# Low weight parts on GpSimd, values by DMA, decay in the keys, and longer pauses in a two-layer hybrid decoder step

## The chip, the cores and the metric

The kernel runs on one core of one Trainium2 chip. The metric is the device time of one execution in microseconds; the time of a kernel is the median of its runs. The core's engines are named as in the profile: PE is TensorE's matrix products, PEld its weight loads, DVE is VectorE, ACT is ScalarE, POOL is GpSimd and SP is the engine that issues most of the DMAs. Each engine works through its own queue in order.

## The reference

The reference is one inference step of two decoder layers for a prompt of 512 tokens and 8 samples of 4 tokens, which share the weights: 544 tokens in all, 1024 channels. A layer does the following (cut to what matters here):

```python
h = rmsnorm(x, norm1_g) * (1 + scale1) + shift1
z = h @ w_in                       # columns for four mixers and for four merge gates
yA = pool_mixer(z_A)               # causal means over 2, 4, 8, 16 tokens
yB = retention(z_B)                # rotary queries and keys, decay, chunks of 128
yC = B * conv3(C * h_c)            # short gated convolution
yD = rwkv7_mixer(z_D)              # the scan, below
mixed = sum(sigmoid(z_gate[n]) * (y[n] @ w_br[n]) for n in A, B, C, D) @ w_out
x = x + gate1 * mixed
h2 = rmsnorm(x, norm2_g) * (1 + scale2) + shift2
up = causal_dwconv3(h2 @ w_up)
x = x + gate2 * ((silu(up_a) * up_b) @ w_down)
```

The scan of branch D carries one 64 x 64 state per head over the tokens, for 4 heads:

```python
def step(S, inp):
    rt, wt, kt, vt, at, bt = inp
    S = S * wt + (S @ at)[:, None] * bt + vt[:, None] * kt     # decay, delta rule, value x key
    return S, S @ rt
```

Besides the output rows the step returns the new states of every mixer.

## The kernel before

Channels lie on the 128 partitions, tokens along the free dimension. The 544 tokens are worked in two halves of 272 columns (`HS`), so one weight block of 128 x 128 multiplies 272 columns at a time.

**The weight stream.** All large weights of a layer come in 138 units (`NU`) of 128 x 1024, in the order in which they are used: 8 units for branch D's input (`RW_UNITS`), 6 for branch C (`SC_UNITS`), 10 for branch C's gates and projection, 2 for branch A (`PO_UNITS`), 10 for A's gates, 8 for branch B (`RET_UNITS`), 10 for D's gates, 10 for B's gates, 8 for the output projection, and the rest for the feed-forward part. Units 0 to 63 are the mixing weights. `load_unit` (L104) fetches a unit by DMA into `raw` (three buffers), lets ScalarE round it to a high part `whi` (L113) and lets VectorE subtract to get the low part `wlo` (L114); two units of layer 0 have this subtraction on GpSimd. `getw` calls it two or three units ahead of their use. Activations are split in the same way (`split_hilo`). `mm3` then forms three products for each block: high by high (L133), high by low (L134), low by high (L135), into a PSUM bank of the pool `psd` (three banks).

**The planner.** The order of TensorE's instructions is written out by hand: it is the order of the program. The other engines' instructions are put in order by a scheduler that knows priorities. Work with small matmuls (the branch D mixer `rwkv`, retention, the conditioning products `ada`, the norms) is written as Python generators. After each `mm3` the function `slot` looks which generators are due; a generator says by `yield n` after how many more of the large products it wants to go on. So a pause is a number of large products; as `slot` is asked after every third, a pause of 16 lasts 18.

**Branch D.** `rwkv` first forms decays and keys (L404 to L450). `products(T)` makes, for each block of 128 tokens, the scaled keys `bkv` (L481) and the scaled `LG` (L473, L475) on VectorE, with a few columns copied by GpSimd (L474); five blocks follow one another at pauses of 48 and 44. In each, small matmuls turn the keys (L500, into `BK`) and multiply them (L507). A triangular system is solved by substitution on VectorE (L568 to L580) and comes back through DRAM into `XT`. Then the scan runs over 16 chunks of 32 tokens. A chunk has three steps, parted by the pauses `D_G`, `D_S` and `D_P`:

1. a matmul with the state and values `Z` (L653), whose result four copies bring to `gs` (two on ScalarE, two on VectorE, L615);
2. a matmul with `XT` (L620), whose result four copies write into `Z` (L624); `newZ` (L600) prepares the `Z` of the next pair of chunks: GpSimd clears blocks and VectorE copies the values `vT` into their places, 32 x 64 each (L607);
3. the matmuls of the new state (L673) and the outputs (L677); VectorE adds the decayed old state `Pn` (L685), multiplies by the decay `dec` and writes the halves into `Z` (L691); GpSimd forms `Pn` for the next chunk (L692).

Behind the scan come the 8 x 4 sample tokens (L712 to L751), a norm over each head (L759, L383 to L391) and the split that the projection of branch D's gates reads (L775, L395). The retention of branch B starts when the scan is done (`M["scan_done"]`).

**The ends of the two halves of a layer.** `residual` (L341) adds a product to the stream `x`: VectorE reads the PSUM bank for the prompt columns (L346) and, in the second half, for the 32 sample columns (L350), whose result `t` stands in a buffer of the pool `zr`. That pool has ten buffers of 562 columns and serves nearly every intermediate: norms, gates, convolutions, keys.

Where the merge gates run, `gates` lets ScalarE take the sigmoid of a unit's product (L1129), VectorE multiply the projected branch by it (L1111) and GpSimd or VectorE add it up (L1113).

Of the kernel before, what the change touches and what calls it, by code (L numbers as in the profile page):

```python
# [10 lines left out]
F32 = mybir.dt.float32  # L11
# [13 lines left out]
NU = 138  # L25
D_G, D_S, D_P = 12, 12, 18
KAPPA = -math.exp(-0.5)
# [16 lines left out]
def tile_hybrid_step(ctx: ExitStack, tc: tile.TileContext, io: dict):  # L44
# [11 lines left out]
    t4p = ctx.enter_context(tc.tile_pool(name="t4p", bufs=14))  # L56
    zrp = ctx.enter_context(tc.tile_pool(name="zrp", bufs=10))
    wp = ctx.enter_context(tc.tile_pool(name="wp", bufs=4))
    drp = ctx.enter_context(tc.tile_pool(name="drp", bufs=2, space=bass.MemoryType.DRAM))
# [6 lines left out]
    def ZR(n=562, dt=F32):  # L66
        return zrp.tile([128, n], dt, tag="zr", name=nm("zr"))

    def PM():
# [34 lines left out]
    def load_unit(l, u):  # L104
        raw = wp.tile([128, 1024], F32, tag="raw", name=nm("raw"), bufs=3)
        nc.sync.dma_start(raw, io["wst"][l, u])
        dst = extra_pools.get((l, u))
        if dst is None:
            hi = wp.tile([128, 1024], F32R, tag="whi", name=nm("whi"))
            lo = wp.tile([128, 1024], F32R, tag="wlo", name=nm("wlo"))  # L110
        else:
            hi, lo = dst()
        S.copy(hi, raw)  # L113
        (G if (l, u) in ((0, 1), (0, 2)) else V).tensor_tensor(out=lo, in0=raw, in1=hi, op=SUB)  # L114
        wloaded[(l, u)] = (hi, lo)
# [225 lines left out]
    def residual(xt, m, ps, half, gate):  # L341
        c0, c1 = HS[half]
        npc = HALF if half == 0 else SEQ - HALF
        x = xk(xt, m)
        with tc.high_priority():
            V.scalar_tensor_tensor(out=x[:, c0:c0 + npc], in0=ps[:, :npc], scalar=gate[:, m, 0:1], in1=x[:, c0:c0 + npc],  # L346
                                   op0=MUL, op1=ADD)
            if half == 1:
                t = ZR(32)
                V.tensor_tensor(out=smp(t), in0=smp(ps[:, npc:HALF]),  # L350
                                in1=gate[:, m, 1:9].unsqueeze(2).broadcast_to([128, NB, DT]), op=MUL)
        if half == 1:
            V.tensor_tensor(out=x[:, SEQ:TOK], in0=x[:, SEQ:TOK], in1=t, op=ADD)
        return x[:, c0:c1]
# [42 lines left out]
    def rwkv(l, za, zb, M, yD):  # L397
# [51 lines left out]
        def products(T):  # L449
# [29 lines left out]
            for w, src in enumerate((kkb, za)):  # L479
                for p in range(2):  # L480
                    V.tensor_tensor(out=bkv[:, p, :, w ^ p, :], in0=src[:, 2 + p, t0:t0 + n].rearrange("p (c t) -> p c t", t=32),  # L481
                                    in1=Ei[:, p, :].rearrange("p (c t) -> p c t", t=32), op=MUL)
            return bkv

        bkn = products(0)
        yield 48, True
        for T in range(5):
            n = 128 if T < 4 else 32
            nch = n // 32
            bkv = bkn  # L490
            if T < 4:
# [3 lines left out]
            for c in range(nch):  # L495
                for p in range(2):
                    cc = (c * 2 + p) * 64
                    for q in range(2):
                        r = par_rows(q)
                        PE.matmul(psB[kv_rows(q), cc:cc + 64], lhsT=bkv[r, p, c].rearrange("r w t -> r (w t)"),  # L500
                                  rhs=ident[r, 64 * q:64 * q + 64], start=True, stop=True)
# [21 lines left out]
            if T < 4:  # L523
                yield 44, True
        rks = []
# [74 lines left out]
        def newZ(blocks):  # L600

            Z = [M["pool"].tile([128, 2, 2, 64], F32, tag=f"z{q}", name=nm("z"), bufs=2) for q in range(2)]
            for q in range(2):
                for p in range(2):
                    G.memset(Z[q][b_rows(q, p), :, p, :], 0.0)
                    for c, (vT, j) in enumerate(blocks):
                        V.tensor_copy(Z[q][k_rows(q, p), c, p, :], vT[32 * j:32 * j + 32, p, q, :])  # L607
            return Z
# [31 lines left out]
        for q in range(2):  # L640
            G.memset(Z[q][par_rows(q), 0], 0.0)
        Pn = None
        P0 = None
        g0s = None
        yield 42
        for ch in range(16):
# [28 lines left out]
            for p in range(2):  # L675
                for q in range(2):
                    PE.matmul(pY[par_rows(q), p, 32 * c:32 * c + 32], lhsT=Z[q][:, c % 2, p, :], rhs=LG[q][:, ch, p, r_cols(q)],  # L677
                              start=True, stop=True)
            pP = psP[:, 0:128].rearrange("r (p i) -> r p i", p=2)
            db = dec[:, :, ch:ch + 1].broadcast_to([128, 2, 64])  # L680
            Pt = M["pool"].tile([128, 2, 64], F32, tag="pt", name=nm("pt"), bufs=2)
            if Pn is None:
                V.tensor_copy(Pt, pP)
            else:
                V.tensor_tensor(out=Pt, in0=pP, in1=Pn, op=ADD)  # L685
            Pn = M["pool"].tile([128, 2, 64], F32, tag="pn", name=nm("pn"), bufs=2)
            if ch < 15:
                Zt, cn = (Z, 1) if c % 2 == 0 else (Zn, 0)
                for q in range(2):
                    r = par_rows(q)  # L690
                    V.tensor_tensor(out=Zt[q][r, cn], in0=Pt[r], in1=db[r], op=MUL)  # L691
            G.tensor_tensor(out=Pn, in0=Pt, in1=db, op=MUL)  # L692
            if c == 3:
# [3 lines left out]
            if ch == 14:  # L697
                psG0 = PM()
                g0v = psG0[:, 0:128].rearrange("r (p w b t) -> r p w b t", p=2, w=2, t=DT)
                for p in range(2):  # L700
                    for b in range(NB):
                        for q in range(2):
# [3 lines left out]
                                      start=True, stop=True)  # L706
                g0 = ZR(128)
                S.copy(g0, psG0[:, 0:128])
# [71 lines left out]
    def retention(l, p, rt, M, yB):  # L780
# [36 lines left out]
        for T in range(4):  # L817
            for q in range(2):
                PE.matmul(pst[par_rows(q), 64 * T:64 * T + 64], lhsT=kt[:, T, par_rows(q)], rhs=vt[:, T, par_rows(q)],
                          start=True, stop=True)  # L820
        sms_s = ZR(32)
        V.tensor_tensor(out=sms_s[0:64], in0=ps[0:64, 0:32], in1=cst[0:64, C_RETS:C_RETS + 32], op=MUL)
        vks = ZR(128)
        S.copy(vks[0:64], pv[0:64, 0:128])
# [744 lines left out]
```

## Time and profile before

| | |
|---|---|
| median of 3 runs | 1979.79 us (1979.74 to 1980.87) |
| the profiled execution | 1977.9 us |
| its span | 1976.1 us |
| granted TensorE clock, mean over the span | 0.99 |
| DMA, mean over the span | 115 GB/s |

The profile is of one execution. A row of a timeline names start, duration, engine, line, operation, output from input and shape; in square brackets stands the idle time of the engine before it and what ended that. A row of the waits names who waited for whom, the total, the number of times and the longest. A row of a group adds up all instructions of one line and names; its last column is the idle time of the engine ahead of them. Buffer numbers are left out: `zr` is any buffer of that pool, `pd` a bank of `psd`, `pm` one of the pool for small matmuls, `t` one of fourteen large buffers.

### The profile page before, as it was taken

How to read it: one execution, taken by the hardware profiler on the slowest of the kernel's cores; microseconds unless marked ns; L12 is line 12 of the kernel's file. 1: busy time of each engine (PE TensorE's matmuls, PEld its weight loads, DVE VectorE, ACT ScalarE, POOL GpSimd, SP SyncE). 2: the span in 40 equal slices, each digit the busy share in tenths (PEclk: the TensorE clock that was granted, in tenths of full speed). 3: DMA queues.
4: the chain of work that ended last, by engine and by line, in shares of the span. 5: the costliest groups of instructions: out<-in, count | busy, mean ns of one | idle time of the engine just before them, and what ended most of it. 6: DMA issues, size and time to landing. Idle time of an engine off the chain costs nothing.

```text
span 1976.1 us, 39220 instructions
## 1 busy us (share of the span) xinstructions
PE 1908.5 (97%) x16188; PEld 1829.6 (93%) x16188; DVE 1111.4 (56%) x2267; ACT 831.2 (42%) x1581; POOL 315.7 (16%) x627
## 2 busy tenths in 40 slices
PE   5999999999999999999999999999999999999997
PEld 4989888899999998899989899889999999999997
DVE  5466654643565653455673667556335765455565
ACT  4642332452445531435455433326424555243542
POOL 2120123213001210112201201232210012011210
PEclk8999999999999999999999999999999999999998
DMA  7323434423342257622332132124224222222231
GB/s 311 98 87 112 139 117 149 141 82 95 125 148 104 91 205 291 234 86 86 120 130 66 57 106 68 65 95 127 76 85 163 72 80 93 86 86 86 90 101 46
DMA packets 75555, 227.16 MB, mean 115 GB/s; under 512 B 20208, under 2 KB 23072, under 8 KB 73584
## 3 DMA queue, kind: packets, MB, share of 16 engines
q1 hardware_dynamic: 69872, 210.43, 31.9%
q0 software_dynamic: 3536, 11.53, 1.7%
q10 hardware_dynamic: 1968, 2.69, 0.5%
q8 instruction: 127, 2.08, 0.4%
q14 instruction: 52, 0.43, 0.1%
HBM read 213.33 MB, written 9.06 MB: 113 GB/s over the span
## 4 chain that ended last, share of the span: by engine, by line
PE 90%; DVE 5%; ACT 2%; DMA 1%; issue 1%; DVEq 0%; ACTq 0%
PE pd L133 27%; PE pd L135 26%; PE pd L134 26%; PE pm L236 2%; DVE wlo L114 1%; PE pm L673 1%; ACT whi L113 1%; DMA raw<-in_wst 1%; PE pm L500 1%; PE pm L677 1%; PE pm L653 0%; DMA t<-in_wada 0%; PE pm L507 0%; PE pm L620 0%; PE pm L383 0%
## 5 line engine op out<-in xcount | busy, mean ns | idle before, releaser
L133 PE MATMUL pd<-t,whi 128*128 128x272 f32 x4104 | 1207.3, 294 | 7.5 <-DVE zr L350 3.6
L135 PE MATMUL pd<-t,wlo 128*128 128x272 f32 x4104 | 1187.5, 289 | 0.0
L134 PE MATMUL pd<-t,whi 128*128 128x272 f32 x4104 | 1181.8, 288 | 0.1
L133 PEld LDWEIGHTS pd<-t,whi 128*128 128x128 f32 x4104 | 773.9, 189 | 39.9 <-issue 26.4
L134 PEld LDWEIGHTS pd<-t,whi 128*128 128x128 f32 x4104 | 775.7, 189 | 1.3 <-DVE t L395 0.3
L135 PEld LDWEIGHTS pd<-t,wlo 128*128 128x128 f32 x4104 | 774.3, 189 | 0.0
L114 DVE TENSOR_TENSOR wlo<-raw,whi 128x1024 fp32r<-128x1024 f32 x256 | 316.9, 1238 | 301.7 <-ACT whi L113 301.4
L113 ACT CAST whi<-raw 128x1024 fp32r<-128x1024 f32 x258 | 270.5, 1049 | 433.4 <-PE pd L134 419.6
L1276 POOL COPY off<-zr 128x18 f32<-128x18 f32 x88 | 76.2, 866 | 558.8 <-ACT zr L1274 558.8
L346 DVE SCALAR_TENSOR_TENSOR t<-pd,mod,t 128x272 f32<-128x272 f32 (+1 forms) x160 | 76.9, 481 | 112.5 <-PE pd L135 111.6
L1274 ACT COPY zr<-pd 128x272 f32<-128x272 f32 (+2 forms) x264 | 72.7, 311 | 78.4 <-PE pd L135 78.4
L1129 ACT ACTIVATE zr<-pd 128x272 f32<-128x272 f32 x128 | 50.3, 395 | 110.3 <-PE pd L135 106.2
L1111 DVE TENSOR_TENSOR zr<-pd,zr 128x272 f32<-128x272 f32 x96 | 41.1, 437 | 98.8 <-PE pd L135 98.1
L1113 POOL TENSOR_TENSOR t<-t,zr 128x272 f32<-128x272 f32 x64 | 71.3, 1133 | 112.5 <-DVE zr L1111 112.4
L1040 DVE SCALAR_TENSOR_TENSOR zr<-zr,par,zr 128x560 f32<-128x560 f32 x92 | 73.4, 800 | 10.0 <-ACT zr L1039 9.9
L1041 DVE SCALAR_TENSOR_TENSOR zr<-zr,par,zr 128x560 f32<-128x560 f32 x92 | 73.4, 801 | 2.8
L1039 ACT ACTIVATE zr<-zr,par 128x560 f32<-128x560 f32 x92 | 70.2, 765 | 6.8
L394 ACT CAST t<-zr 128x544 fp32r<-128x544 f32 (+1 forms) x96 | 49.5, 530 | 53.4 <-DVE zr L1287 53.0
L395 DVE TENSOR_TENSOR t<-zr,t 128x544 fp32r<-128x544 f32 (+1 forms) x96 | 54.5, 580 | 30.7 <-ACT t L394 30.4
L276 ACT ACTIVATE zr<-t 128x272 f32<-128x272 f32 (+1 forms) x72 | 32.2, 455 | 82.8 <-DVE t L346 54.6
L133 PE MATMUL pd<-t,t 128*128 128x272 f32 x224 | 64.8, 289 | 0.2
L134 PE MATMUL pd<-t,t 128*128 128x272 f32 x224 | 64.5, 288 | 0.0
(283 smaller groups left out, 1770.1 us busy)
## 6 DMA issues: line engine op xcount, KB each, us to landing
raw<-in_wst SPq DMA_DIRECT2D x276, 512.0 KB, 3.4
t<-in_wada SPq DMA_DIRECT2D x32, 1024.0 KB, 9.5
raw<-in_wada SPq DMA_DIRECT2D x24, 512.0 KB, 3.4
zr<-in_rope POOLq DMA_DIRECT2D x16, 272.0 KB, 3.6
t<-in_wada SPq DMA_DIRECT2D x8, 512.0 KB, 6.1
t<-in_xT SPq DMA_DIRECT2D x4, 544.0 KB, 6.1
zr<-zr ACTq DMA_DIRECT2D x32, 68.0 KB, 2.9
t<-in_xT SPq DMA_DIRECT2D x2, 1088.0 KB, 7.1
```

What stands on the lines that cost most here:

```text
L113: S.copy(hi, raw)
L114: (G if (l, u) in ((0, 1), (0, 2)) else V).tensor_tensor(out=lo, in0=raw, in1=hi, op=SUB)
L133: PE.matmul(ps, lhsT=a, rhs=xh, start=first, stop=False)
L134: PE.matmul(ps, lhsT=a, rhs=xl, start=False, stop=False)
L135: PE.matmul(ps, lhsT=b, rhs=xh, start=False, stop=last)
L346: V.scalar_tensor_tensor(out=x[:, c0:c0 + npc], in0=ps[:, :npc], scalar=gate[:, m, 0:1], in1=x[:, c0:c0 + npc], op0=MUL, op1=ADD)
L1039: S.activation(cv, u[:, 0:560], AF.Copy, scale=wcol(0))
L1040: V.scalar_tensor_tensor(out=cv, in0=u[:, 1:561], scalar=wcol(1), in1=cv, op0=MUL, op1=ADD)
L1041: V.scalar_tensor_tensor(out=cv, in0=u[:, 2:562], scalar=wcol(2), in1=cv, op0=MUL, op1=ADD)
L1113: (V if last else G).tensor_tensor(out=a[:, c0:c1], in0=a[:, c0:c1], in1=gs, op=ADD)
L1274: pad_evac(lambda o, i, sl: S.copy(o, i), u, ps, half, 2)
L1276: G.tensor_copy(off[:, 22 * s + j], u[:, 512:562].rearrange("p (x t) -> p x t", t=2)[:, 0:25:3, :])
```

## The change

- **Low parts.** The subtraction of L114 goes to GpSimd for every unit below `UP0` = 64 in both layers, but for units 0 and 3 of layer 0: 126 units, where two had it before.
- **Values by DMA.** In `newZ` the copies of the values (L607) become DMAs on SP's queue: 8 for a `Z` of two chunks, 4 for the last.
- **Decay in the keys.** `products` multiplies the scaled keys of the prompt blocks by the decay of their chunk into a further buffer `bkd`, and the matmuls that turn the keys (L500) read that. In the scan the new state then goes from PSUM, with the decayed old state `Eo` added, straight into `Z`, one half of the rows at a time; GpSimd multiplies what stands in `Z` by the next chunk's decay into `E`. The last chunk writes `Pn` by one sum.
- **Own buffers.** A pool `zsp` of five small buffers (`ZS`) takes `t` of `residual`, `g0`, and two small results of retention.
- **Pauses.** `D_G`, `D_S`, `D_P` go from 12, 12, 18 to 16, 16, 20; the pause after the first `products` from 48 to 60 and those between blocks from 44 to 56.

```diff
-D_G, D_S, D_P = 12, 12, 18
+UP0 = 64
+D_G, D_S, D_P = 16, 16, 20
...
+    zsp = ctx.enter_context(tc.tile_pool(name="zsp", bufs=5))
...
+    def ZS(n):
+        return zsp.tile([128, n], F32, tag="zs", name=nm("zs"))
...
-        (G if (l, u) in ((0, 1), (0, 2)) else V).tensor_tensor(out=lo, in0=raw, in1=hi, op=SUB)
+        (G if u < UP0 and (l, u) not in ((0, 0), (0, 3)) else V).tensor_tensor(out=lo, in0=raw, in1=hi, op=SUB)
...
-                t = ZR(32)
+                t = ZS(32)
...
-            return bkv
+
+            bkd = ZR(512)
+            bkdv = bkd[:, 0:4 * n].rearrange("p (q c x) -> p q c x", q=2, x=64)
+            if T < 4:
+                V.tensor_tensor(out=bkdv, in0=bkv.rearrange("p q c w t -> p q c (w t)"),
+                                in1=dec[:, :, 4 * T:4 * T + nch].unsqueeze(3).broadcast_to([128, 2, nch, 64]), op=MUL)
+            return bkv, bkdv if T < 4 else bkv.rearrange("p q c w t -> p q c (w t)")
 
         bkn = products(0)
-        yield 48, True
+        yield 60, True
...
-                        PE.matmul(psB[kv_rows(q), cc:cc + 64], lhsT=bkv[r, p, c].rearrange("r w t -> r (w t)"),
+                        PE.matmul(psB[kv_rows(q), cc:cc + 64], lhsT=bkd[r, p, c],
                                   rhs=ident[r, 64 * q:64 * q + 64], start=True, stop=True)
...
-                yield 44, True
+                yield 56, True
...
-                        V.tensor_copy(Z[q][k_rows(q, p), c, p, :], vT[32 * j:32 * j + 32, p, q, :])
+                        nc.sync.dma_start(Z[q][k_rows(q, p), c, p, :], vT[32 * j:32 * j + 32, p, q, :])
...
-            pP = psP[:, 0:128].rearrange("r (p i) -> r p i", p=2)
-            db = dec[:, :, ch:ch + 1].broadcast_to([128, 2, 64])
-            Pt = M["pool"].tile([128, 2, 64], F32, tag="pt", name=nm("pt"), bufs=2)
-            if Pn is None:
-                V.tensor_copy(Pt, pP)
-            else:
-                V.tensor_tensor(out=Pt, in0=pP, in1=Pn, op=ADD)
-            Pn = M["pool"].tile([128, 2, 64], F32, tag="pn", name=nm("pn"), bufs=2)
             if ch < 15:
                 Zt, cn = (Z, 1) if c % 2 == 0 else (Zn, 0)
+                E = M["pool"].tile([128, 2, 64], F32, tag="pt", name=nm("pt"), bufs=2)
                 for q in range(2):
                     r = par_rows(q)
-                    V.tensor_tensor(out=Zt[q][r, cn], in0=Pt[r], in1=db[r], op=MUL)
-            G.tensor_tensor(out=Pn, in0=Pt, in1=db, op=MUL)
+                    pP = psP[r, 0:128].rearrange("r (p i) -> r p i", p=2)
+                    if ch:
+                        V.tensor_tensor(out=Zt[q][r, cn], in0=pP, in1=Eo[r], op=ADD)
+                    else:
+                        V.tensor_copy(Zt[q][r, cn], pP)
+                    G.tensor_tensor(out=E[r], in0=Zt[q][r, cn], in1=dec[r, :, ch + 1:ch + 2].broadcast_to([64, 2, 64]), op=MUL)
+                Eo = E
+            else:
+                Pn = M["pool"].tile([128, 2, 64], F32, tag="pn", name=nm("pn"), bufs=1)
+                V.tensor_tensor(out=Pn, in0=psP[:, 0:128].rearrange("r (p i) -> r p i", p=2), in1=Eo, op=ADD)
...
-                g0 = ZR(128)
+                g0 = ZS(128)
...
-        sms_s = ZR(32)
+        sms_s = ZS(32)
...
-        vks = ZR(128)
+        vks = ZS(128)
```

More of the change, by code (lines that the diff above doesn't have):

```diff
@@ L489, in rwkv @@
             nch = n // 32
-            bkv = bkn
+            bkv, bkd = bkn
             if T < 4:
@@ L641, in rwkv @@
             G.memset(Z[q][par_rows(q), 0], 0.0)
-        Pn = None
+        Eo = None
         P0 = None
```

## The prediction, made before the changed kernel ran

> **What bounds the kernel now.** I read the page's engine totals first, then the chain that ended last, then what TensorE waited for, then timelines around those waits.
>
> ```profile
> span 1976.1 us, 39220 instructions
> PE 1908.5 (97%) x16188; PEld 1829.6 (93%) x16188; DVE 1111.4 (56%) x2267; ACT 831.2 (42%) x1581; POOL 315.7 (16%) x627
> ...
> PE 90%; DVE 5%; ACT 2%; DMA 1%; issue 1%; DVEq 0%; ACTq 0%
> ```
>
> TensorE is busy 97% of the span and owns 90% of the chain. The change removes no product from TensorE, so it can only move the waits between products. The pace of the stream comes from a timeline of TensorE: the first and the last of 24 weight products in a row.
>
> ```profile
> 1002.72 0.29 PE L133 MATMUL pd<-t,whi 128*128 128x272 f32 x1
> ...
> 1005.63 0.29 PE L135 MATMUL pd<-t,wlo 128*128 128x272 f32 x1
> ```
>
> That is 2.91 us for 23 steps, 0.1265 us a product: the unit in which the pauses of the planner (`D_G` and the others) count. Next, TensorE's waits over the whole run (waiting line, releaser: total us, times, longest):
>
> ```profile
> PE pm L287 <- DVE zr L279: 14.9, 3, 12.4
> PE pm L620 <- DVE gs L615: 10.4, 10, 1.3
> PE pm L500 <- DVE zr L481: 8.4, 3, 4.0
> PE pd L133 <- DVE zr L350: 8.2, 6, 2.8
> PE pd L133 <- DVE zr L1111: 2.5, 2, 1.2
> ```
>
> L287 is almost all start-up, which the change leaves alone. Three waits are in its reach: the scan's L620 (10.4 us), the products stage's L500 (8.4 us) and the residual's L350 (8.2 us): 27.0 us, 1.4% of the span, is all that can be won.
>
> **Term A, the scan (L620).** VectorE around one such wait:
>
> ```profile
> 270.70 1.23 DVE L114 TENSOR_TENSOR wlo<-raw,whi 128x1024 fp32r<-128x1024 f32 x1 [2.83 <-ACT whi L113]
> 271.84 0.78 DVE L1111 TENSOR_TENSOR zr<-pd,zr 128x272 f32<-128x272 f32 x2
> 272.65 0.46 DVE L615 COPY gs<-pm 32x64 f32<-32x64 f32 x2
> ```
>
> The scan's copies `gs` stand behind a low part (1.23 us) and, because of it, behind two gate products (0.78 us). The change takes the low part off VectorE, and `D_G` 12 to 16 gives the copies more time: the planner is asked every third product, so 12 becomes 18, 6 x 0.1265 = 0.76 us. The longest wait, 1.3 us, is shorter than 1.23 + 0.76. I keep about a fifth (pool and rotary stages, where VectorE still has long operations): 10.4 to 1.9, **-8.5 us** (between -10.4 and 0).
>
> The scan's own operations (line, buffers, count, busy, mean ns, idle before):
>
> ```profile
> L607 DVE COPY z<-vt 32x64 f32<-32x64 f32 x136 | 28.5, 210 | 2.6
> L691 DVE TENSOR_TENSOR z<-pt,dec 64x128 f32<-64x128 f32 x60 | 20.8, 347 | 1.6
> L685 DVE TENSOR_TENSOR pt<-pm,pn 128x128 f32<-128x128 f32 x30 | 8.7, 292 | 20.6 <-PE pm L673 20.5
> L692 POOL TENSOR_TENSOR pn<-pt,dec 128x128 f32<-128x128 f32 x32 | 15.3, 479 | 101.7 <-DVE pt L685 57.8 <-DVE pt L683 43.8
> ```
>
> With the decay in the keys, VectorE's state update falls from one sum and two products (292 + 2 x 347 = 986 ns) to two sums of half the rows (at most 2 x 292). It hides behind the pause before the next chunk (`D_P`, 18 products, 2.3 us), where TensorE waits for nothing now, so I count zero; without that cover it would be a gain of 0.4 us a chunk. GpSimd's product becomes two of at most 479 ns. VectorE's next sum waits for them, one chunk later: 57 products, 7.2 us. Queued with them on GpSimd are, in that time, a low part or two (2.45 us each, below), adds and memsets; they fit, so zero.
>
> **Term B, the products stage (L500).** TensorE and VectorE at the first wait:
>
> ```profile
> 114.19 0.33 PE L500 MATMUL pm<-cst,zr 64*64 64x64 f32 x4
> 118.14 1.03 PE L500 MATMUL pm<-cst,zr 64*64 64x64 f32 x28 [3.62 <-DVE zr L481]
> ```
>
> ```profile
> 117.15 0.42 DVE L475 TENSOR_TENSOR t<-t,zr 64x256 f32<-64x256 f32 x1
> 117.59 0.49 DVE L481 TENSOR_TENSOR zr<-t,zr 128x128 f32<-128x128 f32 x2
> ```
>
> VectorE ends the first block's keys at 118.08; TensorE came at 114.2. Now the pause goes from 48 to 60, 12 x 0.1265 = 1.52 us later: a gain of 1.52 us a layer. The new product with the decay is 128x512; by the other products of SBUF operands (64x256 in 0.42 us) some 0.65 us, an estimate, once on this path per layer. And a low part on GpSimd falls into this stretch. What that does, the start-up shows, where two low parts run on GpSimd already; first GpSimd, then VectorE:
>
> ```profile
> 20.96 3.61 POOL L114 TENSOR_TENSOR wlo<-raw,whi 128x1024 fp32r<-128x1024 f32 x1 [6.24 <-ACT whi L113]
> 26.67 2.45 POOL L114 TENSOR_TENSOR wlo<-raw,whi 128x1024 fp32r<-128x1024 f32 x1 [2.10 <-ACT whi L113]
> ```
>
> ```profile
> 22.29 0.17 DVE L214 TENSOR_TENSOR mod<-pm,par 128x18 f32<-128x18 f32 x1
> 22.38 2.49 DVE L942 TENSOR_TENSOR t<-t,zr 128x272 f32<-128x272 f32 x1
> 24.87 0.43 DVE L942 TENSOR_TENSOR t<-t,zr 128x272 f32<-128x272 f32 x1
> ```
>
> A low part takes 2.45 us on GpSimd, against 1.23 on VectorE. While the first ran (20.96 to 24.57), an L942 of VectorE, two SBUF operands, took 2.49 us instead of 0.43 and ended just behind it; L214, which reads PSUM, took its usual 0.17. So a low part on GpSimd can hold VectorE for 0 to 2.45 us. I take half, 1.2 us a layer. Term B: 2 x (-1.52 + 0.65 + 1.2) = **+0.7 us** (between -1.7 and +3.2).
>
> [...]
>
> **Term C, the residual (L350).** VectorE at the layer change:
>
> ```profile
> 1008.06 0.46 DVE L346 SCALAR_TENSOR_TENSOR t<-pd,mod,t 128x240 f32<-128x240 f32 x1
> ...
> 1012.59 0.46 DVE L346 SCALAR_TENSOR_TENSOR t<-pd,mod,t 128x240 f32<-128x240 f32 x1
> ...
> 1014.84 0.18 DVE L350 TENSOR_TENSOR zr<-pd,mod 128x32 f32<-128x32 f32 x1
> ```
>
> Three L346 run before the first L350 follows, which belongs to the first of them: its 32-column result needs one of the ten `zr` buffers, all taken by the norm. Until then three PSUM banks stay held, and TensorE waits 2.8 us. With a buffer of its own (`ZS`) L350 can follow L346 at once. I read 8.2 us in six waits: 2.3 us behind each output projection, 3.6 at the layer change. But VectorE is nearly full there and becomes the next limit, through the norm's sums. Behind the output projection I take 1.5 of 2.3 us, twice. At the layer change five low parts of the next layer (6.1 us of VectorE) go to GpSimd, where they hold its SBUF work instead; bounds -3.6 and +6.1 (five times 2.45 - 1.23), and I take -1.5, nearer to the row that shows the buffer. Term C: **-4.5 us** (-8.2 to +6.1).
>
> **Term D, the later end of the scan.** Per layer the pauses add 306 products (12, 12, 18 become 18, 18, 21: 15 in each of 16 chunks, 6 behind them; 12, and four times 12, in the products stage): the scan ends 38.7 us later. From the start of that work to its last step the pauses add up to 1488 products now, 1794 then. The branch-D projection that reads it stands at product 1872 from there (at 48 a unit and 480 a branch's gates: 6 units, 480, 2 units, 480, 8 units, then 3 gate units). The work behind the last matmuls now:
>
> ```profile
> 365.01 1.83 PE pm L383 x8
> ```
>
> ```profile
> 375.52 0.72 DVE L395 TENSOR_TENSOR t<-t,t 128x544 fp32r<-128x544 f32 x1
> ```
>
> 11.2 us. The L383 step comes at 1785, 87 products or 11.0 us and its own 1.83 us ahead of the projection: it just fits, so zero for the wait itself. But the norms of the scan and of both retention halves now all fall among the sigmoids of the gates, where ScalarE changes tables between sigmoid, logarithm and exponential, 1.28 us a load:
>
> ```profile
> 432.66 1.28 ACT L391 ACT_TABLE_LOAD   x1
> ```
>
> ```profile
> 434.64 0.73 DVE L872 TENSOR_TENSOR t<-t,zr 128x544 f32<-128x544 f32 x1 [6.35 <-ACT zr L391]
> ```
>
> VectorE stands 6.35 us at L872, with the gate product L1111 behind it; that is the 2.5 us of L1111 in TensorE's waits, one retention half a layer. Now two halves meet the gates: **+2.5 us** (0 to +8).
>
> **Term E, the values by DMA.** 136 copies of 210 ns leave VectorE (counted in A) and become as many small transfers on SP's queue. The nearest rows, SP's small copies (SP timeline; issues with us to landing) and its waits:
>
> ```profile
> 195.48 1.49 SPq L586 DMA_DIRECT2D t<-scr  x3
> ```
>
> ```profile
> t<-scr SPq DMA_DIRECT2D x8, 64.0 KB, 2.8
> ```
>
> ```profile
> SPq L106 <- DVE wlo L114: 1088.2, 178, 27.2
> ```
>
> Eight cost 4.0 us to issue and land 2.8 us later, 6.8 us. The first set of a layer has 42 products, 5.3 us, the others some 96, 12.1 us: 1 us a layer, **+2.0 us**. Behind a weight load that waits (6.1 us on average) the first set would be 6.1 + 6.8 - 5.3 = 7.6 us late: bounds 0 and +15. Weights behind the copies lose nothing: they are loaded units ahead.
>
> **The sum** against the profiled execution's own 1977.9 us (span 1976.1): -8.5 + 0.7 - 4.5 + 2.5 + 2.0 = -7.8, so 1970.1. The runs' median, 1979.79, is 1.9 above that execution: **1972 us**, 0.4% faster. A difference under 0.2%, 4 us, can't be told from none here.
>
> **Rivals.**
> 1. [...] For: L942. Against: the scan's copies and sums read PSUM, like L214, and GpSimd's load is 16%. If low parts on GpSimd meet two-SBUF work in most places, A gains nothing (rotary and pool operations are stopped ahead of the copies), B is +3.2, the layer change +6.1 against -3.0 behind the output projections, D and E stay: +10.8, 1991 us. [...] Slower; chance 0.17.
> 2. *The tail is late.* The 11.2 us grow, as retention now runs beside them, and the projection waits: for 5 us a layer more, -7.8 + 10 = +2.2: 1982 us, the same. For: the fit is within 2 us. Against: retention's matmuls also hold TensorE back. Chance 0.12.
> 3. *It does not do what it says.* ScalarE's half of `gs`, behind weight casts (1.05 us), sets the copies, and VectorE's norm work keeps L350's wait: A and C give a third: -4.3 + 5.2, 1981 us, the same. Against: the L615 row stands behind VectorE's own work. Chance 0.11.
>
> **How the numbers follow.** Forecast 0.60, with its own range 1959 to 1976; rivals 0.17, 0.12, 0.11. Faster 0.60, same 0.23, slower 0.17. The low end takes A, B and C at their good ends and D, E at zero (-20.3, 1959.5); the high end reaches most of the way into rival 1: 1959 to 1988.
>
> **What would show it.** Right: L620 under 3 us and L350 near zero in TensorE's waits; L500 near 8; L114 on GpSimd some 126 times at 2.5 to 3.6 us. Wrong: VectorE's two-SBUF groups with means far up and L500 or L287 grown (rival 1); TensorE waiting for the split of branch D (rival 2); waits on a DMA of `z` (term E too small); products waiting for `wlo` from GpSimd, which I cost at nothing because loads run one to three units (7 us and more) ahead.

## The result, and the profile after

| | before | after |
|---|---|---|
| median of the runs | 1979.76 us (1978.27 to 1980.87) | 2033.02 us (2030.42 to 2038.23) |
| ratio | 1 | 1.0273, interval 1.0251 to 1.0294 |
| profiled execution | 1977.9 us, span 1976.1 | 2033.06 us, span 2031.3 |

The change makes the kernel 53 us slower, 2.7%; 1972 us was forecast, 0.4% faster. Line numbers of the kernel after lie 5 to 12 above those of before: products L138 to L140, low part L119, gate products L1123, keys L492 and L511, substitution L586 and L588, values L618, the scan's `gs` L626 and L631. The page of after, its span, its engine totals and two groups (line, engine, buffers, count, busy, mean ns, idle before):

```profile
span 2031.3 us, 39384 instructions
PE 1925.1 (95%) x16188; PEld 1846.5 (91%) x16188; DVE 1011.0 (50%) x1985; ACT 833.3 (41%) x1583; POOL 590.7 (29%) x779
...
L119 POOL TENSOR_TENSOR wlo<-raw,whi 128x1024 fp32r<-128x1024 f32 x124 | 299.6, 2418 | 398.1 <-ACT whi L118 380.5
```

VectorE's busy time fell by 100 us (1111.4 to 1011.0; a held operation counts as busy: 2.31 us in the row of L588 below, for a step of some 0.24), as the change meant, and TensorE still has the same 16188 products. Yet it waits more. Its waits (waiting line, releaser: total, times, longest):

```profile
PE pm L292 <- DVE zr L284: 21.0, 3, 12.7
PE pm L511 <- DVE zr L492: 13.3, 2, 6.7
PE pm L664 <- DMA z<-vt: 11.0, 4, 3.4
PE pd L138 <- DVE t L1123: 9.7, 4, 3.3
...
PE pm L631 <- DVE gs L626: 8.1, 6, 2.1
PE pm L831 <- ACT t L804: 6.1, 2, 3.1
```

The residual's wait (L350, 8.2 us before) is off the list. The scan, which was to fall below 3 us, fell only from 10.4 to 8.1. Two waits that were to stay about as they were grew: the norms, start-up included (14.9 to 21.0), and the products stage (8.4 to 13.3). The waits for `z`, for L1123 writing `t` and for L804 are new.

A list of waits doesn't add up to a difference of times, so I summed TensorE's lost time by stage: the distance between two starts, less what the same pair of lines needs at its quick end (the quickest fifth), for excesses over 0.13 us, both layers together:

| stage | before | after |
|---|---|---|
| branch C's units, with the products stage | 11.2 | 14.7 |
| branch C's gates, with the substitution | 1.7 | 12.7 |
| branch A's units, where the scan starts | 1.1 | 16.7 |
| branch A's gates, with the scan | 15.3 | 6.9 |
| branch B's units | 11.4 | 9.9 |
| branch D's gates | 5.3 | 23.6 |
| branch B's gates | 0.0 | 3.9 |
| output projection, feed-forward, ends of halves | 34.8 | 25.0 |
| first units of layer 0 / layer 1 | 8.4 / 1.3 | 8.6 / 9.9 |
| all waits | 90.4 | 131.8 |
| products that run at half clock | 8.3 | 24.2 |

Waits make +41.4 us and slow products +15.9; small excesses changed by -2. That is 55.3 us for 55.2 us of span. The last line of the table was in no term of the prediction.

**What holds VectorE.** Groups of VectorE by line, after:

```profile
L284 DVE TENSOR_TENSOR zr<-zr,zr 128x272 f32<-128x272 f32 (+1 forms) x63 | 35.4, 562 | 16.9 <-ACT zr L281 16.0
L586 DVE TENSOR_TENSOR t<-t 128x126 f32<-128x126 f32 (+22 forms) x62 | 26.1, 421 | 2.0 <-DMA t<-in_xinit 0.2
L588 DVE TENSOR_TENSOR t<-t 128x126 f32<-128x126 f32 (+22 forms) x62 | 22.1, 356 | 2.1
L626 DVE COPY gs<-pm 32x64 f32<-32x64 f32 x68 | 15.2, 224 | 86.7 <-ACT gs L626 86.1
L492 DVE TENSOR_TENSOR zr<-zr,dec 128x512 f32<-128x512 f32 x8 | 9.6, 1198 | 0.4
```

and the same of before:

```profile
L279 DVE TENSOR_TENSOR zr<-zr,zr 128x272 f32<-128x272 f32 (+1 forms) x63 | 29.7, 471 | 17.2 <-ACT zr L276 16.4
L577 DVE TENSOR_TENSOR t<-t 128x126 f32<-128x126 f32 (+22 forms) x62 | 15.8, 255 | 2.1
L575 DVE TENSOR_TENSOR t<-t 128x126 f32<-128x126 f32 (+22 forms) x62 | 15.8, 255 | 2.4 <-DMA t<-in_xinit 0.5
L615 DVE COPY gs<-pm 32x64 f32<-32x64 f32 x68 | 15.2, 224 | 25.7 <-ACT gs L615 24.9
```

Work with two SBUF operands has become slower: the substitution's steps from 255 to 421 and 356 ns, the norm's sums from 471 to 562. `gs`, which reads PSUM, takes 224 ns in both. The means hide how it happens: of the 124 substitution steps eight take 2.09 to 2.53 us each, and the others at most 0.30, as before. A timeline of the first layer's branch C gates shows single meetings:

```profile
197.67 4.75 POOL L119 TENSOR_TENSOR wlo<-raw,whi 128x1024 fp32r<-128x1024 f32 x2 [7.23 <-ACT whi L118]
197.87 2.31 DVE L588 TENSOR_TENSOR t<-t 128x70 f32<-128x70 f32 x1
...
200.21 2.27 DVE L586 TENSOR_TENSOR t<-t 128x56 f32<-128x56 f32 x1
...
204.03 0.78 DVE L1123 TENSOR_TENSOR t<-pd,zr 128x272 f32<-128x272 f32 x2
204.52 0.59 PE L138 MATMUL pd<-t,whi 128*128 128x272 f32 x1 [3.30 <-DVE t L1123]
```

Two low parts run on GpSimd from 197.67 to 202.42. Two substitution steps, some 0.24 us each, take 2.31 and 2.27 us and end as the low parts do. By these two holds the gate products L1123 come some 4.1 us late, their PSUM banks stay full, and TensorE waits 3.30 us. Then comes the second price. Windows of the same kernel (stretch, its length, busy time and count of PE, PEld, DVE, ACT, POOL, then PEclk, the granted clock, then the DMA engines' busy share and GB/s):

```profile
190.00:203.80 13.80, 9.52 (x73) 9.02 (x72) 12.84 (x33) 3.19 (x5) 5.19 (x3) 1.00 0.12 39
203.80:210.60 6.80, 6.08 (x27) 6.08 (x28) 0.98 (x4) 0.09 (x1) 0.34 (x2) 0.50 0.75 184
210.60:230.00 19.40, 19.40 (x163) 17.89 (x163) 3.40 (x10) 5.10 (x9) 5.84 (x3) 1.00 0.35 100
```

From the last 0.7 us of the wait on, TensorE is at half clock for 6.8 us, most of which VectorE and GpSimd stand idle. In the clock's record of the whole trace the half-clock stretches sum to 40.9 us before and 96.7 us after. Of the 13 stretches of after between the start and the end, nine stand at a wait of over 3 us and three among shorter ones (1.3 to 2.1 us); one, like two of before, has no wait above 0.3 us near it.

At the layer change the meeting costs most. Rows of VectorE, GpSimd and TensorE:

```profile
1056.82 2.34 POOL L119 TENSOR_TENSOR t<-raw,t 128x1024 fp32r<-128x1024 f32 x1 [7.89 <-ACT t L118]
1057.04 2.42 DVE L284 TENSOR_TENSOR zr<-zr,zr 128x272 f32<-128x272 f32 x1
1059.12 2.54 POOL L119 TENSOR_TENSOR t<-raw,t 128x1024 fp32r<-128x1024 f32 x1
1059.56 2.39 DVE L284 TENSOR_TENSOR zr<-zr,zr 128x272 f32<-128x272 f32 x1
...
1062.01 1.27 PE L292 MATMUL pm<-zr,cst 128*128 128x272 f32 x2 [6.39 <-DVE zr L284]
```

Two sums of some 0.44 us take 2.42 and 2.39 us, one behind each of two low parts in a row, and TensorE waits 6.39 us. The first of them ends at 1059.46, behind the first low part, though the second has begun at 1059.12: the held operation gets its turn between the two, and the next one is held anew.

### The profile page after: what moved, and what is told of

It reads as the page before. It is cut to its first block, busy times and chain, and to the rows that moved or that the text cites. A ratio compares the mean times of both kernels' runs of the same rounds, so it can differ in the third digit from the quotient of the medians.

```text
span 2031.3 us, 39384 instructions
## 1 busy us (share of the span) xinstructions
PE 1925.1 (95%) x16188; PEld 1846.5 (91%) x16188; DVE 1011.0 (50%) x1985; ACT 833.3 (41%) x1583; POOL 590.7 (29%) x779
## 5 line engine op out<-in xcount | busy, mean ns | idle before, releaser
L138 PE MATMUL pd<-t,whi 128*128 128x272 f32 x4104 | 1215.7, 296 | 19.8 <-DVE t L1123 9.7
L140 PE MATMUL pd<-t,wlo 128*128 128x272 f32 x4104 | 1194.2, 291 | 0.0
L138 PEld LDWEIGHTS pd<-t,whi 128*128 128x128 f32 x4104 | 781.5, 190 | 55.1 <-issue 23.5
L140 PEld LDWEIGHTS pd<-t,wlo 128*128 128x128 f32 x4104 | 781.5, 190 | 0.0
L119 POOL TENSOR_TENSOR wlo<-raw,whi 128x1024 fp32r<-128x1024 f32 x124 | 299.6, 2418 | 398.1 <-ACT whi L118 380.5
L119 DVE TENSOR_TENSOR wlo<-raw,whi 128x1024 fp32r<-128x1024 f32 x134 | 164.1, 1224 | 202.1 <-ACT whi L118 201.8
L1123 DVE TENSOR_TENSOR zr<-pd,zr 128x272 f32<-128x272 f32 x96 | 42.0, 439 | 131.5 <-PE pd L140 130.6
L1052 DVE SCALAR_TENSOR_TENSOR zr<-zr,par,zr 128x560 f32<-128x560 f32 x92 | 77.9, 849 | 12.2 <-ACT zr L1051 12.1
L1053 DVE SCALAR_TENSOR_TENSOR zr<-zr,par,zr 128x560 f32<-128x560 f32 x92 | 73.5, 801 | 2.8
L140 PE MATMUL pd<-t,t 128*128 128x272 f32 x224 | 64.6, 288 | 0.0
L138 PE MATMUL pd<-t,t 128*128 128x272 f32 x224 | 64.6, 288 | 0.0
L139 PE MATMUL pd<-t,t 128*128 128x272 f32 x224 | 64.4, 287 | 0.0
```

Of the source, the lines that this page charges most:

```text
L119: (G if u < UP0 and (l, u) not in ((0, 0), (0, 3)) else V).tensor_tensor(out=lo, in0=raw, in1=hi, op=SUB)
L138: PE.matmul(ps, lhsT=a, rhs=xh, start=first, stop=False)
L139: PE.matmul(ps, lhsT=a, rhs=xl, start=False, stop=False)
L140: PE.matmul(ps, lhsT=b, rhs=xh, start=False, stop=last)
L1052: V.scalar_tensor_tensor(out=cv, in0=u[:, 1:561], scalar=wcol(1), in1=cv, op0=MUL, op1=ADD)
L1053: V.scalar_tensor_tensor(out=cv, in0=u[:, 2:562], scalar=wcol(2), in1=cv, op0=MUL, op1=ADD)
```

## The experiments

The change has five parts. In this order of undoing, each step is one run against its neighbour (ratio to the kernel before, with interval):

| kernel | ratio | step |
|---|---|---|
| before + own buffers (e5) | 0.9942 (0.9927 to 0.9957) | -11.5 us |
| + decay in the keys (e6) | 0.9951 (0.9936 to 0.9966) | +1.8 |
| + values by DMA (e7) | 1.0014 (1.0004 to 1.0023) | +12.5 |
| + longer pauses (e1) | 1.0057 (1.0040 to 1.0074) | +8.5 |
| + low parts on GpSimd (the change) | 1.0273 (1.0251 to 1.0294) | +42.8 |

A step is the difference of two ratios times 1979.8 us; by the intervals it is known to about 4 us, so the keys' 1.8 can't be told from none.

### The low parts

**e1**, the changed kernel with the low parts where they were:

```diff
-        (G if u < UP0 and (l, u) not in ((0, 0), (0, 3)) else V).tensor_tensor(out=lo, ...)
+        (G if (l, u) in ((0, 1), (0, 2)) else V).tensor_tensor(out=lo, ...)
```

> The changed kernel (2033) with the low parts back on VectorE (two stay on GpSimd, as before). [...] Rival, the values by DMA and the late tail make the loss: 2020 or more, with the waits for L1123 in the branch-C gates still there.

Measured: 1991.18 us (1990.17 to 1991.43), 42 us less than the changed kernel. For the case that GpSimd's low parts hold VectorE, with half clock behind TensorE's long waits, I had put it at 1995 to 2005 us; it came 4 us below. The waits in branch C's gates are back at 1.7 us, the substitution's groups at 255 ns, and the scan's wait is all but gone:

```profile
PE pm L631 <- DVE gs L626: 0.3, 2, 0.2
```

So, beside the other parts, four fifths of the loss are the low parts on GpSimd; and the scan's gain, which the prediction gave to them, comes without them.

**e4**, the kernel before with the same one line the other way.

> The kernel before with only the low parts of units below 64 on GpSimd. [...] Rival (the low parts only free VectorE, and the loss needs the other parts): 1970 to 1980.

Measured: 2010.71 us (2010.31 to 2012.01), ratio 1.0159 (1.0143 to 1.0174): +31 us by that line alone, +43 beside the other parts. For the case that the low parts hold VectorE I had put it 15 to 35 us slower, at 1995 to 2015 us; it lies inside. The scan's wait, which it was to shorten, grew:

```profile
PE pm L621 <- DVE gs L616: 12.0, 8, 3.6
PE pd L134 <- DVE zr L351: 12.0, 8, 4.5
PE pm L501 <- DVE zr L482: 11.2, 2, 5.6
PE pd L134 <- DVE t L1112: 7.3, 4, 2.4
```

Why a low part off VectorE doesn't free the scan's copies, the changed kernel shows at 249 us, in branch A's units:

```profile
248.88 2.60 POOL L119 TENSOR_TENSOR wlo<-raw,whi 128x1024 fp32r<-128x1024 f32 x1 [1.15 <-PE pm L664]
249.16 2.37 DVE L1185 SCALAR_TENSOR_TENSOR zr<-t,cst 64x32 f32<-64x32 f32 x1
...
252.43 0.46 DVE L626 COPY gs<-pm 32x64 f32<-32x64 f32 x2
...
253.04 0.41 PE L631 MATMUL pm<-gs,t 128*128 128x64 f32 x2 [1.93 <-DVE gs L626]
```

L1185 is an operation on 64 x 32 values of two SBUF operands, 0.25 us elsewhere. It is held 2.37 us, and `gs` stands behind it in VectorE's queue. The PSUM readers weren't held themselves (`gs` took 217 to 231 ns, and none of the 713 operations of VectorE that read PSUM over 0.70 us), but they queue behind what is: before, 1.23 us of low part; now, 2.4 us of a held operation. The three next longest of these six waits (398, 1270 and 1412 us) have one ahead of `gs` too, of 2.87, 2.68 and 2.90 us, from the pool mixer or the rotary step.

**e9**, the changed kernel with the low parts of units 14 to 26 alone back on VectorE.

```diff
-        (G if u < UP0 and (l, u) ...
+        (G if u < UP0 and not 14 <= u <= 26 and (l, u) ...
```

> The changed kernel with 26 of the 124 low parts back on VectorE: those of units 14 to 26, loaded while the scan's substitution steps (two SBUF operands) run beside branch C's gates. Theory (the low parts on GpSimd cost where VectorE's two-SBUF work stands behind them, and the substitution is half of it: TensorE's idle time in that stage is 20 us in the changed kernel and 3 with all low parts on VectorE): 2010 to 2018 us, the stage back to 3 to 5 us. Rival (a low part on GpSimd costs about the same wherever it runs, 42 us over 124, so 26 of them are worth 9): 2022 to 2026 us.

Measured: 2013.32 us (2011.38 to 2013.46), ratio 1.0165 (1.0150 to 1.0181). 26 of 124 low parts carry 20 of the 42 us. By the count of the table the waits of branch C's gates fell from 12.7 to 1.7 us and the 5.0 us lost there at half clock are gone, 16 us together; the products stage, ahead of which the first of these units are loaded, gave back 4.0 more (L511, 13.3 to 9.3). The substitution's steps are as before:

```profile
L588 DVE TENSOR_TENSOR t<-t 128x126 f32<-128x126 f32 (+22 forms) x62 | 15.8, 256 | 2.1
```

The cost lies in the place, not in the count: where a long chain of small two-SBUF steps stands ahead of the gate products.

### The waits and the clock

**e8**, the kernel before with six stops of TensorE put into the second layer's feed-forward.

```diff
+    def stand(k):
+        ps = PM()
+        t = ZR(TOK)
+        PE.matmul(ps[:, 0:128], lhsT=ident, rhs=ident, ...)
+        V.tensor_copy(t[:, 0:128], ps[:, 0:128])
+        for _ in range(k):
+            V.tensor_tensor(out=t[:, 0:128], in0=t[:, 0:128], in1=ident, op=MUL)
+        PE.matmul(ps[:, 128:256], lhsT=ident, rhs=t[:, 0:128], ...)
+        V.tensor_copy(t[:, 128:256], ps[:, 128:256])
...
+                if l == 1 and (part, m) in DOSE:
+                    stand(DOSE[(part, m)])
```

> The kernel before with six added stops of TensorE in the second layer's feed-forward, where it hardly ever waits: a small matmul, then a chain of 2, 12, 4, 16, 6 and 9 small products on VectorE, then a small matmul that needs their result. By a VectorE product of some 0.2 us and about 0.6 us for the ends the stops last about 1, 3, 1.4, 4, 1.8 and 2.5 us, 14 us together. Theory (a stop of about 3 us or more is followed by a stretch of half clock, multiples of 3.4 us, shorter ones are not): half clock behind the stops of 12 and 16 products alone, and the time grows by the stops plus about half of these stretches, 17 to 22 us. Rival (the half clock has another cause and only goes with the long stops of the changed kernel): no new stretch at half clock, time grows by the stops alone, 12 to 16 us.

Measured: 2026.10 us (2024.05 to 2026.66), +46. The stops came out longer than planned, since VectorE had other work queued ahead. TensorE's rows at four of them (the wait in brackets), and windows behind three:

```profile
1703.79 0.49 PE L897 MATMUL pm<-zr,cst 128*128 128x128 f32 x2 [2.58 <-DVE zr L896]
...
1734.25 0.79 PE L897 MATMUL pm<-zr,cst 128*128 128x128 f32 x2 [5.84 <-DVE zr L896]
...
1807.51 0.49 PE L897 MATMUL pm<-zr,cst 128*128 128x128 f32 x2 [3.86 <-DVE zr L896]
...
1822.90 0.80 PE L897 MATMUL pm<-zr,cst 128*128 128x128 f32 x2 [7.15 <-DVE zr L896]
```

```profile
1704.00:1714.90 10.90, 10.90 (x89) 10.90 (x89) 3.28 (x7) 1.05 (x1) 0.00 (x0) 1.00 0.25 82
1807.90:1811.30 3.40, 3.40 (x17) 3.40 (x17) 0.79 (x2) 0.00 (x0) 0.00 (x0) 0.50 0.19 74
1811.30:1815.30 4.00, 4.00 (x34) 4.00 (x33) 1.26 (x4) 0.00 (x0) 0.00 (x0) 1.00 0.00 0
1734.60:1739.60 5.00, 5.00 (x24) 5.00 (x23) 0.29 (x1) 0.00 (x0) 0.00 (x0) 0.50 0.02 3
```

Behind the stop of 2.58 us the clock stayed at 1.00, with 89 products in 10.9 us. Behind 3.86 us it was 0.50 for 3.4 us, 17 products instead of some 28; the stops of 4.51 to 7.15 us all have such a stretch, 6.8 to 10.2 us in the clock's record, 5.4 to 6.1 of it behind the stop's end. The six waits sum to 29.6 us; 25.8 us at half clock behind five of them cost half, 12.9; together 42.5 of the 46. Nearly all of the rest is no stop of the six: at the layer change the wait for L350 of 2.82 us, which is in the kernel before too, has 6.8 us at half clock behind it here (from 1016.0 us) and had none there, half of which is 3.4. So the theory holds for these stops: the one of 2.58 us cost itself alone, the five of 3.86 to 7.15 us cost themselves and those 12.9 us more, 2.6 us on average; the wait of 2.82 us went either way. The rival, stops alone, would have left 16 us unexplained.

The changed kernel has such stretches at shorter waits than 3.86 us too: 3.4 us at its two waits of 3.06 us and 6.8 us at its two of 3.30 us. In the clock's record of both kernels every stretch between the start and the end is 3.4, 6.8 or 10.2 us long.

### The values by DMA

**e2**, the changed kernel with `V.tensor_copy` in the place of the DMA in `newZ`.

> The changed kernel with the values copied by VectorE again instead of by DMA. Theory 1 (values by DMA cost the first set of each layer, 4.6 and 6.8 us, and a window of 6.8 us at half clock behind each): 2033 - 11 - 7 = about 2015. Rival, the transfers are hidden and the wait for them only stands in for another: within 4 us of 2033.

Measured: 2030.89 us (2026.88 to 2036.12), the change's time less 2. The theory failed here: the wait for `z` is gone, but the scan's L631 grew from 8.1 to 14.8 us and L1123 from 9.7 to 14.2, since 136 copies are back in a VectorE queue that the low parts hold up (an explanation from the code; no run separates it). The rival is right.

**e7 and e6** tell the price where nothing is held: the changed kernel with low parts on VectorE and short pauses, with the values by DMA (e7) and by VectorE (e6).

> The changed kernel with the low parts on VectorE, short pauses and the values copied by VectorE: only the decay in the keys and the own buffers are left. Theory (the decay in the keys costs its extra product, about 0.65 us a layer, and frees VectorE of some 0.4 us a chunk, all hidden): within 2 us of the kernel with own buffers alone. Rival (the added product and the two-sided hand-over with GpSimd lengthen the recurrence, or GpSimd's small products hold VectorE): 4 us or more above it.

> The changed kernel with the low parts on VectorE and short pauses: keys, own buffers and the values by DMA are left. The difference to the kernel with keys and buffers is the price of the values by DMA by itself. Theory (with short pauses the transfers have even less time, so TensorE waits for them at the start of the scan, but the copies gone from VectorE give as much back, as in the changed kernel, where the copies back on VectorE gave 2 us): within 4 us of it. Rival (the wait for the first transfers is all cost once VectorE has no low parts to be relieved of): 5 to 12 us above it.

Measured: 1970.24 us (1968.67 to 1971.57) for e6 and 1982.34 us (1980.30 to 1986.48) for e7: +12, the rival. SP and TensorE of e7 at the first set:

```profile
210.59 10.10 SPq L618 DMA_DIRECT2D z<-vt  x16
```

```profile
217.57 0.46 PE L664 MATMUL pm<-z,t 128*128 128x128 f32 x2 [2.00 <-DMA z<-vt]
...
221.36 0.77 PE L664 MATMUL pm<-z,t 128*128 128x128 f32 x2 [3.33 <-DMA z<-vt]
```

Two sets are issued back to back, 16 in 10.10 us, and the second matmul of the first chunk runs when they are nearly through, 5.3 us of waits in all. They stand together, and half clock follows: 6.8 us behind the first set of each layer, 13.7 of the 22.3 us that the whole trace has more than e6 (57.1 and 34.8).

**e10**, e7 with 96 products instead of 42 ahead of the first chunk (`yield 42` to `yield 96`).

> The kernel with keys, own buffers and the values by DMA (1982 us), with the pause before the scan's first chunk raised from 42 to 96 products (6.8 us), which comes after the first values are issued. Theory (the values by DMA cost in one place, the first set of each layer, 5.7 and 6.0 us of TensorE's idle time there and the half clock behind it): the waits for z are gone and the time is back at 1966 to 1973 us. Rival (the transfers cost all along the scan, behind weight loads): 1977 to 1983 us.

Measured: 1975.17 us (1969.84 to 1984.85), ratio 0.9982 (0.9966 to 0.9997), between both expectations. The waits for `z` are gone and half clock is at 39.4 us, so the place was right; 5.4 us came back as waits of the state update for the scan's own copies (L684 for `z`, L635), and 3.5 us in retention.

### The pauses

**e3**, the changed kernel with the pauses of before.

```diff
-D_G, D_S, D_P = 16, 16, 20
+D_G, D_S, D_P = 12, 12, 18
...
-        yield 60, True
+        yield 48, True
...
-                yield 56, True
+                yield 44, True
```

> The changed kernel with the pauses of before (12, 12, 18; 48; 44). Theory 1 (the late end of the scan puts its norm and both retention halves among the gates of D: TensorE's waits there grew by 25 us, four half-clock windows of 3.4 to 6.8 us behind them): minus 25 to 33, plus 5 for the scan's L631 waits that come back: 2005 to 2013. Rival, the D-gate waits come from low parts on GpSimd: 2025 or more.

Measured: 2005.35 us (2002.61 to 2017.77), ratio 1.0143 (1.0109 to 1.0176): 28 us faster than the change, and branch D's gates wait 5.0 us instead of 23.6. **e12** asks why, with the kernel before and one number: `yield 42` ahead of the scan becomes `yield 348`, so that all of it ends 306 products later while no pause inside it grows.

> The kernel before with one number changed: the pause ahead of the scan's first chunk is 348 products instead of 42, so that the scan ends 306 products (38.7 us) later, as with the change's pauses, while every pause inside it stays. Theory (the longer pauses cost through where the scan ends: retention starts behind it and then runs among branch D's gates): TensorE's idle time in that stage grows from 3.2 us to some 15 a layer, as in the changed kernel, and nothing else is relieved, 1996 to 2010 us. Rival (the longer pauses cost where they stand, inside the scan): the stage stays at 3 to 5 us and the time at 1977 to 1986 us.

Measured: 2006.22 us (1999.02 to 2008.08), ratio 1.0127 (1.0102 to 1.0151). Branch D's gates wait 20.2 us (5.3 before), with the change's new wait among them, here under its old numbers (L819, L792):

```profile
PE pm L819 <- ACT t L792: 6.1, 2, 3.1
```

So where the scan ends costs: retention starts behind it and then works among the sigmoids. Not all of the 26 us lie there: branch B's units, into which the scan now reaches, wait 14.1 us (11.4 before) and lose 7 us more at half clock. ScalarE ahead of L819's wait:

```profile
442.39 1.05 ACT L113 CAST whi<-raw 128x1024 fp32r<-128x1024 f32 x1 [2.29 <-PE pd L134]
443.46 1.28 ACT L1129 ACT_TABLE_LOAD   x1
444.75 0.40 ACT L1129 ACTIVATE zr<-pd 128x272 f32<-128x272 f32 x1
445.05 0.64 ACT L394 CAST t<-t 128x544 fp32r<-128x544 f32 x1
445.58 1.08 ACT L792 COPY t<-pm 128x512 f32<-128x512 f32 x2
```

Retention's copy L792 stands behind a weight cast, a table load, a sigmoid and the split of the scan's own result. That is 3.07 us of wait in one piece; at the same wait in the changed kernel (L831, 3.06 us) the clock was halved for 3.4 us.

**e11** asks whether pauses pay if the end doesn't move: before with own buffers, `yield 48` to 84, `D_G` 15, `D_P` 15.

> The kernel before with the own buffers, and pauses that are moved more than lengthened: 84 products instead of 48 ahead of the first products' matmuls, 15 instead of 12 ahead of the scan's answer, 15 instead of 18 behind the state update (36 more in a layer, where the change has 306). Theory (longer pauses pay where the wait stands, and cost only through the later end of the scan, which 36 products don't reach): the wait of the products stage (8.4 us, and 10 us at half clock behind it) and most of the scan's 10.7 us go, 1945 to 1956 us. Rival (the shorter pause behind the state update turns into a wait of its own, or the later scan meets the gates of branch D all the same): 1960 to 1970 us.

Measured: 1972.15 us (1971.58 to 1972.71), ratio 0.9960 (0.9945 to 0.9975), no better than own buffers alone. That is nearer to the rival, but by another way: the products stage no longer waits itself, but branch C's units do, at the same place behind the same VectorE queue:

```profile
1105.36 0.74 DVE L1079 TENSOR_TENSOR zr<-pd,zr 128x272 f32<-128x272 f32 x2
1105.84 0.19 PEld L137 LDWEIGHTS pd<-t,whi 128*128 128x128 f32 x1 [3.80 <-DVE zr L1079]
```

### Own buffers alone

**e5**, the kernel before with the pool `zsp` for the five small results, nothing else.

> The kernel before with one part of the change alone: the five small results have buffers of their own. Theory (term C's mechanism is right, only its price in the changed kernel was hidden by the other parts): TensorE's waits for L350 (8.2 us before) are gone and little takes their place, 1970 to 1975 us. Rival (VectorE's norm work is the next limit and keeps TensorE waiting at the same places): 1977 to 1981 us.

Measured: 1968.47 us (1966.62 to 1970.16), ratio 0.9942 (0.9927 to 0.9957). L350's wait is gone. Behind the output projections nothing takes its place: by the table's count 7.8 us lost there become 2.0. At the layer change it is replaced: 5.4 us lost before and 5.4 after, now as waits for the norm (L291, 2.0 us) and for a split (L398, 1.1 us), with 6.8 us at half clock (from 1024.1 us) that were not there before. The other gain is in branch B's units, 11.4 to 7.1: the sample tokens' products (L742, 2.1 us of waits before) no longer wait for L728, which needed a `zr` buffer while `g0` held one. The two profiled executions differ by 7.7 us only, the medians by 11.5; what makes the other 4 is not shown. It is the fastest version measured, within noise of e6.

## Why the prediction was wrong, point by point

- **Term C, first half: right in kind, too small.** With `t` in its own buffer L350 no longer waits. I took 3.0 of 4.6 us behind the output projections and 1.5 of 3.6 at the layer change; alone it is worth 11.5 us by the medians. "VectorE is nearly full there and becomes the next limit" held at the layer change, more than I allowed: nothing was won there (e5). What failed is to carry it over to the output projections, where 5.8 us went, and to price the other small buffers at nothing: with `g0` in its own buffer branch B's units lose 4.3 us less.
- **Term A (-8.5): right wait, wrong cause.** L620's 10.4 us became 8.1, not 1.9. "The change takes the low part off VectorE" was the failing step: the low part still stops VectorE, from GpSimd, by the two-operand steps of the pool mixer and the rotary stage ahead of `gs`, which took 2.37 to 2.90 us with the hold. The pauses and the values do relieve the scan: 11.6 us in e6, 6.4 with the values by DMA (e7), 0.3 with the pauses too (e1).
- **Terms B and C, the meetings.** "A low part on GpSimd can hold VectorE for 0 to 2.45 us" was read rightly from the start-up's L942. What failed is the list of places: two products stages and the layer change, with the substitution never named. This is the step that turned the sign: the sum has 2.4 us for the low parts in the products stages and a net gain at the layer change, and the low parts cost 42.8. The substitution's 124 steps of 0.25 us run beside branch C's gates with the gate products in the same queue, and 16 us of the cost lay there (e9). A place is no single hold either: at the layer change two low parts in a row held one sum each. In the products stage each of the three sizes can be told. The pause's 1.52 us held: from e7 to e1 the two stops at L511 shrank from 5.1 and 6.3 us to 3.6 and 4.8. The low parts, from e1 to the change, added 4.9 us (8.4 to 13.3) where I had 2.4. And the product with the decay took 0.69 us undisturbed (0.65 estimated), but the wait grew by 3.0 us in e6 (8.4 to 11.4) and not by 1.3, as other operations of VectorE came ahead of the keys in a new order (a low part of 1.21 us at the first stop).
- **Term D (+2.5, 0 to +8).** The pauses cost 8.5 us net, and 28 us beside the low parts. "It just fits, so zero for the wait itself" asked only whether the projection waits for the split. It doesn't; retention's own small matmuls do (L831, L856), and TensorE stands for them in order. I counted the norms behind a table load and not the copies that feed matmuls.
- **Term E (+2.0, 0 to +15).** Inside its bounds, mis-sized: 12.5 us. "1 us a layer" counted eight transfers at 0.50 us; the queue issued 16 in a row at 0.63 us, and the chunk waited some 5.5 us a layer (11.0 in e7).
- **Costed at nothing, rightly:** products never wait for `wlo` from GpSimd; no such line is among TensorE's waits.
- **A term that was missing.** Each wait was priced at its own length. Half clock behind the long ones cost 16 us of the 55; the stretches in the trace of before (clock 0.990 over the span) would have shown it: 13.7 us in the start-up, 3.4 us at L500's wait of 3.62 us and 6.8 at that of 4.00 us.
- **Rival 1** named the cause, low parts that meet two-SBUF work, and put it at 1991 us with a chance of .17. It fell short by 42 us: the substitution, the clock, and terms D and E left at their small values. Its measure, in how many places they meet, was the wrong one: e9 shows that a fifth of the low parts carried half of the cost. Its argument against itself, that PSUM readers pass, held for the operations (at most 0.70 us) and not for the queue.
- **Rivals 2 and 3.** Rival 2 had the right place, branch D's gates (5.3 to 23.6 us), but not the wait: TensorE stands there for retention's matmuls and not for the split. Rival 3's sign, a wait for L350 that stays, did not come.

Still open is why the low parts cost 43 us in the changed kernel and 31 in the kernel before (e4); the waits there may be longer and go with half clock more often, but no run separates this.

## What to carry to other kernels

Moving the low parts to an idle engine wasn't free: it cost 31 us alone (e4) and 42.8 beside the other parts, as steps of VectorE on two SBUF operands were held beside them, 2.1 to 2.5 us each in the substitution. So list every chain of such steps that would run beside a moved operation, and who queues behind that chain, before counting the work that left. A longer pause moves everything behind it, so look at what stage the end falls into and which small matmuls there hold TensorE. And look at the granted clock behind each long wait before pricing it: behind the five stops of 3.86 to 7.15 us in e8, half clock cost 2.6 us on average on top of their length.

## What the runs showed of the hardware that I had not expected

- Half clock came with single waits inside an otherwise full stream: in e8 none behind 2.58 us, 3.4 us of it behind 3.86 us, up to 10.2 us at a stop of 7.15 us. The length of the wait alone doesn't tell: the wait of 2.82 us at the layer change had none behind it in the kernel before and 6.8 us in e8, in the changed kernel a wait of 2.1 us among small matmuls has 3.4 us of it, and the stretches of 3.4 us with no wait near them, two before and one after, stay unexplained.
- An operation of VectorE that a low part on GpSimd held got its turn when that one ended, even where the next followed at once: beside two low parts in a row (2.34 and 2.54 us) two sums took 2.42 and 2.39 us, and two substitution steps 2.31 and 2.27. So here each low part held one operation for about its own length, and of the chain of 124 substitution steps eight were held, for 2.09 to 2.53 us each; the others took at most 0.30.
- Small transfers were issued at 0.63 us each (16 in 10.10 us), against 0.50 us in the row the prediction used (three in 1.49 us).
